# The last pooling products at set places, the first projection groups in pairs, and LayerNorm's TensorE steps 12 to 24 products sooner

## The chip, the cores and the metric

The kernel runs on one core of one Trainium2 chip. The metric is the device time of one launch in microseconds (us), taken as the median of three runs: 1085.06 us before the change, from 1084.37 to 1085.12.

## What is computed

One layer of a decoder trunk, in float32, on 288 tokens: 256 of a prompt and 8 x 4 sampled ones. Cut to what matters:

```python
h = rmsnorm(x, norm1_g)                                   # 2048 channels
proj = h @ w_in + b_in
a, gate, z = proj[:, :1024], proj[:, 1024:2048], proj[:, 2048:]
u = a * sigmoid(gate)                                     # after the history of 30 tokens
c = silu(layernorm(depthwise_conv31(u), ln_g, ln_b))
d = mean of z over windows of 2, 4, 8, 16 tokens (one a group of 256 channels) - z
p = (d of each group @ pool_w of the group) * pool_scale
x = x + concat(c, p) @ w_out                              # 2048 x 2048
x = x + relu(rmsnorm(x, norm2_g) @ w_ff1) ** 2 @ w_ff2    # 2048 x 8192 x 2048
y = rmsnorm(x, norm_f)
```

## The kernel before

Channels lie on the 128 partitions, tokens in the free dimension. Each float32 operand of a large product is split into a high part (`whi`, `hh`) that TensorE's float32r keeps, and the rest (`wlo`, `hl`); of the four partial products three are taken. So every product here is one matmul of 128 x 128 weights with 128 x 288 moving values, and all that matters below is called a *product* in that sense.

A group of products is one call of `gemm(banks, rhs)`. Weights come in blocks of 512 KB: SP's queue loads a block (`load`), ScalarE casts the high part (L274), VectorE or GpSimd subtracts for the low part (L279, L282). `ready` holds the weight groups that are already asked for; `gemm` takes the first one and, when it has recorded its products, asks for one more. The stages stand in `SEQUENCE`: c0 to c7 are the eight convolution groups (96 products each, `a` and `gate` of 128 channels), p3 to p0 the projections of the pooling groups, P3 to P0 the 12 products of each pooling group with its own weights (`pool_products`, tile `pp`). The names of the tail are these:

- *g0 to g7*, the first half of `w_out`: eight groups of 48 products each, moving operand `mixp` (tiles `dx`, what `pool_products` wrote), two accumulating banks a group from the pool `acc`, which has room for two groups. VectorE adds the banks to `xT` (L587).
- *h0 to h7*, the second half of `w_out`: eight groups of 48, moving operand `mixc` (tiles `mx`), added at L609.
- *ff1, ff2*: 64 groups of 96 products, 6,144 in all.

LayerNorm needs TensorE three times, and the three places are inside g5 to g7 by `BETWEEN`: `ln_mean` (tile `pmean`, two matmuls in full float32, which take two passes each), `ln_sums` (three thin matmuls into `pt`, L246, then root and reciprocal on ScalarE and VectorE, L249 to L256), and `ln_rows` (three matmuls that spread the result, `pt<-ident,st`). Then VectorE multiplies (`n`, L592), ScalarE does SiLU (L595) and the cast (`mx`, L597), VectorE the low part (L598).

The order of TensorE's instructions comes from two things. While the list `chain` is not empty, `mm` ties every matmul behind the last, so that it stands where the program's text has it. When it is empty, a list scheduler places each instruction by its own estimate. Before the change the chain is given up at P1 (`chain.clear()` at L541), so P1, P0, g0, g1, h0 and h1 lie where the scheduler put them.

A moving operand's high and low parts lie in one tile of four rows of 288 values (L122, `rows`): high parts in rows 1 and 2, low parts in rows 0 and 3. The six products of a pair of channel blocks on one bank read the rows 1, 2, 1, 2, 0, 3: even and odd rows alternate, when nothing comes in between. The string `TURN` is an order for the first 48 products of a group, in which the parity of the row is 1,1,0,1,0,0 four times, then 0,1 six times, then 1,1,0,0 three times; `classes=TURN` reorders the head of a group to it (L332). Before the change it stands in the first stages, at c5, in g2, h2 and in the second group of ff1.

Of the kernel before, what the change touches and what calls it, by code (L numbers as in the profile page):

```python
# [86 lines left out]
def trunk_kernel(ctx: ExitStack, tc: tile.TileContext, io):  # L87
# [46 lines left out]
    def f32(t):  # L134
        return t.bitcast(F32)
# [71 lines left out]
    def load_table(func, src):  # L207

        return nc.scalar.activation(few[: src.shape[0], :], src, func)
# [97 lines left out]
            chain[0] = last.ins  # L307
        return last

    def gemm(banks, rhs, m_outer=False, between={}, classes="", by_part=False):  # L310


        n = len(rhs)
        gets = ready.pop(0)
        todo, begins = [], {}
        if by_part:
            for k in range(0, n, 2):
                sets = [range(len(banks))] if k else [range(2), range(2, len(banks))]
                for last, ms_ in enumerate(sets, 1 - len(sets)):
                    for part, (w, x) in enumerate(((0, 0), (1, 0), (0, 1))):  # L320
                        if last == 0:
                            begins[len(todo)] = (k, None, k + 1)[part]
                        todo += [(k + (1 - d if x else d), m, w, x) for m in ms_ for d in range(2)]
        else:
            pairs = [(k, m) for k in range(0, n, 2) for m in range(len(banks))]
            if m_outer:
                pairs.sort(key=lambda km: km[1])
            for k, m in pairs:
                if m == 0:
                    begins[len(todo)] = k  # L330
                todo += [(k + d, m, w, x) for d, w, x in ((0, 0, 0), (1, 0, 0), (0, 1, 0), (1, 1, 0), (1, 0, 1), (0, 0, 1))]
        head = todo[: len(classes)]  # L332
        for j, c in enumerate(classes):
            todo[j] = next(p for p in head if (p[0] + p[3]) % 2 == int(c))
            head.remove(todo[j])
        ends = {m: [f(j for j, p in enumerate(todo) if p[1] == m) for f in (min, max)] for m in range(len(banks))}
        ahead = None
        for j, (k, m, w, x) in enumerate(todo):
            if begins.get(j) in between:
                ahead = between[begins[j]]()  # L340
            with tc.issue_after(ahead.ins) if ahead is not None and not chain else nullcontext():
                last = mm(banks[m][:, :T], gets[k // 8](k % 8, m)[w], rhs[k][x], start=j == ends[m][0], stop=j == ends[m][1])
        ready.extend(itertools.islice(weights, 1))
        return last.ins
# [4 lines left out]
    def each(bk):  # L349
        return [bk[:, m, :] for m in range(2)]  # L350
# [83 lines left out]
    def conv_products(i, **kw):  # L434
        history(i)
        banks = each(bank2())
        gemm(banks, hx, **kw)
        return banks

    def conv_pair(i, banks):  # L440
        up = u_all[:, i, 0:UO]
        us = samples(u_all[:, i, UO:UL], US)
        ta, gate = [b[:, :T] for b in banks]
        for b in (gate, ta):
            nc.vector.tensor_tensor(b, b, rb, op=ALU.mult)
        tg = tmpp.tile([P, 2, T], F32, name=nm("tg"), tag="ag", bufs=2)[:, 0, :]
        nc.scalar.activation(tg, gate, AF.Sigmoid, bias=v("b_in", 8 + i))
        for out, a, b in ((up[:, CH:UO], ta[:, :SEQ], tg[:, :SEQ]), (us[:, :, CH:US], samples(ta[:, SEQ:T], NS), samples(tg[:, SEQ:T], NS))):
            nc.vector.scalar_tensor_tensor(out=out, in0=a, scalar=v("b_in", i), in1=b, op0=ALU.add, op1=ALU.mult)
        if i % 2 == 0:  # L450
            cs.append(actp.tile([P, 2, T], F32, name=nm("c"), tag="c", bufs=4))
        c = cs[i // 2][:, i % 2, :]
        with later():
            if i % 2 == 0:
                pcs.append(cvp.tile([P, 2, SEQ], F32, name=nm("pc"), tag="cv"))
            pc = pcs[i // 2][:, i % 2, :]
            cwv = vec[:, CWO + i * CW : CWO + (i + 1) * CW]
            nc.scalar.activation(pc, up[:, 0:SEQ], AF.Identity, bias=v("conv_b", i), scale=cwv[:, 0:1])  # L458
            for w in range(1, CW):
                dst = pc if w < CW - 1 else c[:, 0:SEQ]  # L460
                nc.vector.scalar_tensor_tensor(out=dst, in0=up[:, w : w + SEQ], scalar=cwv[:, w : w + 1], in1=pc, op0=ALU.mult, op1=ALU.add)  # L461
            prd = prdp.tile([P, NB, NS, CW + 1], F32, name=nm("prd"), tag="prd")
            nc.scalar.activation(prd[:, :, :, CW], ones[:, 0 : NB * NS].rearrange("p (b t) -> p b t", t=NS), AF.Identity, bias=v("conv_b", i), scale=0.0)
            nc.gpsimd.tensor_tensor(prd[:, :, :, 0:CW], windows(us, CW), cwv[:, None, None, :].to_broadcast([P, NB, NS, CW]), op=ALU.mult)
            cso = c[:, SEQ:T]
            nc.vector.tensor_reduce(samples(cso, NS), prd, axis=AX.X, op=ALU.add)
            if i % 2 and 1 < i < N8 - 1:
                for m in range(2):
                    nc.gpsimd.tensor_tensor(sum_c[:, m, :], (cs[0] if i == 3 else sum_c)[:, m, :], cs[i // 2][:, m, :], op=ALU.add)
            if i == N8 - 2:  # L470
                for part in (sum_c[:, 1, :], c):
                    nc.gpsimd.tensor_tensor(sum_c[:, 0, :], sum_c[:, 0, :], part, op=ALU.add)
# [35 lines left out]
    def pool_products(g):  # L508

        bk = ms("pp")  # L510
        gemm(each(bk), halves(dd[g]))
        for m, (mh, ml) in enumerate(halves(dd[g])):
            i = 2 * g + m
            nc.scalar.activation(mh, bk[:, m, :T], AF.Copy, scale=v("pool_scale", i))
            nc.vector.scalar_tensor_tensor(out=ml, in0=bk[:, m, :T], scalar=v("pool_scale", i), in1=f32(mh), op0=ALU.mult, op1=ALU.subtract)
            mixp[i] = (mh, ml)
# [19 lines left out]
    conv_pair(0, pair0)  # L536
    conv_pair(1, pair1)
    conv_pair(2, third)
    for kind, i in SEQUENCE[3:]:
        if (kind, i) == ("P", 1):  # L540
            chain.clear()  # L541
        if kind == "c":
            conv_pair(i, conv_products(i, classes=TURN if i == 5 else ""))
        elif kind == "p":
            pool_group(i)
        else:
            pool_products(i)
    load_table(AF.Sqrt, f32(mixp[1][0])[:, 0:1])
    with later(2 * LATER):
        nc.sync.dma_start(io["u_out"], u_all[:, :, UO - CH : UL])  # L550
# [25 lines left out]
        norm["rows"], last = spread(norm["sums"])  # L576
        return last

    BETWEEN = {5: {4: ln_mean}, 6: {6: ln_sums}, 7: {2: ln_rows}}
    behind = nullcontext()  # L580
    for g in range(8):
        bk = bank2()
        with behind:
            last = gemm(each(bk), [mixp[k] for k in korder], between=BETWEEN.get(g, {}), classes=TURN if g == 2 else "")
        behind = tc.issue_after(last) if g > 3 else nullcontext()
        x2 = xT[:, 2 * g : 2 * g + 2, :]
        nc.vector.tensor_tensor(x2, x2, bk[:, :, :T], op=ALU.add)  # L587
# [13 lines left out]

    x1 = []
    ss2 = row("ss2")
    last = None
    for g in range(8):
        bk = bank2()
        last = gemm(each(bk), mixc, classes=TURN if g == 2 else "")
        x2 = xT[:, 2 * g : 2 * g + 2, :]
        nc.vector.tensor_tensor(x2, x2, bk[:, :, :T], op=ALU.add)  # L609
        if g < 4:  # L610
            a2 = halves(act2("ax", tag="p", bufs=4))
        elif g < 6:
            if g == 4:
                ax45 = zp.tile([P, N8 * ZL], F32R, name="ax45", tag="z")
                ax45 = ax45[:, 32 : 32 + 8 * T].rearrange("p (g r t) -> p g r t", g=2, r=4)
            a2 = halves(rows(ax45[:, g - 4]))
        else:
            a2 = []
            for m in range(2):
                t2 = actp.tile([P, 2, T], F32R, name=nm("ax"), tag="c", bufs=4)  # L620
                a2.append((t2[:, 1 - m, :], t2[:, m, :]))
        for m, (ah, al) in enumerate(a2):
            k = 2 * g + m
            xk = xT[:, k, :]
            nc.scalar.activation(ah, xk, AF.Copy, scale=v("norm2_g", k))
            nc.vector.scalar_tensor_tensor(out=al, in0=xk, scalar=v("norm2_g", k), in1=f32(ah), op0=ALU.mult, op1=ALU.subtract)
            x1.append((ah, al))
            if k == 0:
                nc.scalar.activation(ss2, xk, AF.Square)
            else:  # L630
                q2 = tmp("q")
                nc.scalar.activation(q2, xk, AF.Square)
                nc.gpsimd.tensor_tensor(ss2, ss2, q2, op=ALU.add)
# [150 lines left out]
```

## Time and profile before

| | |
|---|---|
| median of 3 runs | 1085.06 us (1084.37, 1085.06, 1085.12) |
| span of the profiled execution, first to last instruction | 1082.8 us |
| TensorE busy | 1071.5 us, 8198 matmul records |
| VectorE, ScalarE, GpSimd busy | 635.4, 479.0, 173.6 us |
| granted TensorE clock, mean | 0.997 |
| P1 to the end of h2, the part that the change touches | 159.8 to 239.1 us of the span |

No time of its own is given for the profiled execution beside its span; the three runs lie 1.6 to 2.3 us above it. TensorE counts as busy for nearly the whole span whatever it does, because the records of matmuls overlap (about 0.29 us each, one begun every 0.13 us). So its busy share says little here, and what is to be read is the time from one product's start to the next.

### The profile page before, as it was taken

Reading aid. Unit: us, or ns where it says so; the run is one execution under the profiler, and the core shown is the slowest. Engines: PE = TensorE matmul, PEld = TensorE weight load, DVE = VectorE, ACT = ScalarE, POOL = GpSimd, SP = SyncE. Lnnn points to the kernel's source line nnn. Section 1 sums busy time; section 2 is a strip of 40 time slices with the busy share of each in tenths; the row PEclk is TensorE's granted clock in tenths of the full one; section 3 lists DMA queues with packets and bytes.
Section 4 is the critical chain, followed back from the end, with each engine's and each line's share of the span. In section 5 each row is a group of like instructions: output and inputs, shape, how many; then the busy total and the mean of one; then the engine's idle time right before and its main releaser. Section 6 shows DMA issues by size and latency. Waiting matters only on the chain.

```text
span 1082.8 us, 19572 instructions
## 1 busy us (share of the span) xinstructions
PE 1071.5 (99%) x8198; PEld 1069.9 (99%) x8198; DVE 635.4 (59%) x818; ACT 479.0 (44%) x585; POOL 173.6 (16%) x180
## 2 busy tenths in 40 slices
PE   9999999999999999999999999999999999999996
PEld 9999999999999999999999999999999999999996
DVE  8899999678655544445544444545544445554553
ACT  8654445475544433334443333444433334444441
POOL 0878979512000000000000000000000000000001
PEclk9999999999999999999999999999999999999998
DMA  9896468545555555555555555555555555555522
GB/s 325 281 273 185 137 196 239 176 152 177 173 164 170 172 166 169 174 164 169 171 168 168 175 165 169 174 167 167 174 165 168 174 169 165 173 166 168 173 78 88
DMA packets 58296, 190.71 MB, mean 176 GB/s; under 512 B 6240, under 2 KB 11232, under 8 KB 58208
## 3 DMA queue, kind: packets, MB, share of 16 engines
q1 hardware_dynamic: 56336, 184.35, 53.9%
q0 software_dynamic: 1008, 3.67, 1.9%
q8 instruction: 64, 1.05, 0.4%
q10 hardware_dynamic: 864, 1.44, 0.4%
q14 instruction: 24, 0.20, 0.1%
HBM read 185.16 MB, written 4.28 MB: 175 GB/s over the span
## 4 chain that ended last, share of the span: by engine, by line
PE 77%; issue 20%; ACT 1%; DVE 0%; DMA 0%; POOL 0%; POOLq 0%
PE ac L305 77%; PE pp L305 1%; DMA wr<-in_w 0%; ACT whi L274 0%; POOL xT L720 0%; ACT n L595 0%; DVE wlo L279 0%; PE pt L305 0%; PE pmean L305 0%; POOLq L770 0%; DVE xT L695 0%; DVE n L592 0%; ACT whi L364 0%; ACT mx L597 0%; DVE hx L367 0%
## 5 line engine op out<-in xcount | busy, mean ns | idle before, releaser
L274 ACT CAST whi<-wr 128x1024 fp32r<-128x1024 f32 (+1 forms) x332 | 348.0, 1049 | 551.4 <-PE ac L305 533.5
L279 DVE TENSOR_TENSOR wlo<-wr,whi 128x1024 fp32r<-128x1024 f32 x288 | 353.1, 1226 | 348.5 <-ACT whi L274 348.5
L305 PE MATMUL ac<-ax,whi 128*128 128x288 f32 x2048 | 351.0, 292 | 0.0
L305 PE MATMUL ac<-fx,whi 128*128 128x288 f32 x2048 | 350.2, 292 | 0.0
L305 PEld LDWEIGHTS ac<-ax,whi 128*128 128x128 f32 x2048 | 296.0, 187 | 0.0
L305 PEld LDWEIGHTS ac<-fx,whi 128*128 128x128 f32 x2048 | 295.6, 187 | 0.0
L305 PE MATMUL ac<-ax,wlo 128*128 128x288 f32 x1024 | 217.4, 292 | 0.0
L305 PE MATMUL ac<-fx,wlo 128*128 128x288 f32 x1024 | 216.4, 292 | 0.0
L305 PEld LDWEIGHTS ac<-ax,wlo 128*128 128x128 f32 x1024 | 162.6, 187 | 0.0
L305 PEld LDWEIGHTS ac<-fx,wlo 128*128 128x128 f32 x1024 | 162.3, 187 | 0.0
L305 PE MATMUL ac<-hx,whi 128*128 128x288 f32 x768 | 131.8, 295 | 1.2 <-DVE hx L367 1.2
L720 POOL TENSOR_TENSOR xT<-xT,rf 128x288 f32<-128x288 f32 x4 | 3.1, 795 | 800.1 <-ACT rf L724 800.1
L305 PEld LDWEIGHTS ac<-hx,whi 128*128 128x128 f32 x768 | 112.1, 190 | 1.4 <-ACT hx L369 1.4
L282 POOL TENSOR_TENSOR wlo<-wr,whi 128x512 fp32r<-128x512 f32 x74 | 100.3, 1410 | 35.3 <-ACT whi L274 34.3
L461 DVE SCALAR_TENSOR_TENSOR pc<-u_all,vec,pc 128x256 f32<-128x256 f32 x232 | 99.5, 483 | 1.9 <-ACT pc L458 0.7
L305 PE MATMUL ac<-hx,wlo 128*128 128x288 f32 x384 | 80.1, 294 | 0.0
L305 PEld LDWEIGHTS ac<-hx,wlo 128*128 128x128 f32 x384 | 61.1, 190 | 0.0
L305 PE MATMUL ac<-dx,whi 128*128 128x288 f32 x256 | 46.0, 296 | 0.0
L305 PE MATMUL ac<-mx,whi 128*128 128x288 f32 x256 | 45.1, 294 | 0.1
L664 DVE SCALAR_TENSOR_TENSOR t<-ac,r 128x576 f32<-128x576 f32 x32 | 24.2, 758 | 25.1 <-PE ac L305 25.1
L305 PEld LDWEIGHTS ac<-dx,whi 128*128 128x128 f32 x256 | 38.0, 188 | 0.2
L305 PEld LDWEIGHTS ac<-mx,whi 128*128 128x128 f32 x256 | 37.5, 188 | 0.6 <-ACT mx L597 0.4
(133 smaller groups left out, 533.6 us busy)
## 6 DMA issues: line engine op xcount, KB each, us to landing
wr<-in_w SPq DMA_DIRECT2D x335, 512.0 KB, 3.8
wlo<-in_w POOLq DMA_DIRECT2D x7, 512.0 KB, 7.7
xT<-in_xT SPq DMA_DIRECT2D x8, 288.0 KB, 7.3
wr<-in_w SPq DMA_DIRECT2D x5, 256.0 KB, 3.6
out_u_out<-u_all SPq DMA_DIRECT2D x1, 1208.0 KB, 9.3
u_all<-in_hist_c SPq DMA_DIRECT2D x8, 136.0 KB, 6.2
out_z_out<-z_all SPq DMA_DIRECT2D x1, 668.0 KB, 9.9
z_all<-in_hist_p SPq DMA_DIRECT2D x4, 152.0 KB, 7.5
```

What stands on the lines that cost most here:

```text
L274: nc.scalar.copy(hi, raw)
L279: nc.vector.tensor_tensor(lo, raw, f32(hi), op=ALU.subtract)
L282: nc.gpsimd.tensor_tensor(lo[:, j : j + 2, :], raw[:, j : j + 2, :], f32(hi[:, j : j + 2, :]), op=ALU.subtract)
L305: last = nc.tensor.matmul(*args, **kw)
L461: nc.vector.scalar_tensor_tensor(out=dst, in0=up[:, w : w + SEQ], scalar=cwv[:, w : w + 1], in1=pc, op0=ALU.mult, op1=ALU.add)
L664: nc.vector.scalar_tensor_tensor(out=t, in0=bk[:, :, :T], scalar=0.0, in1=both(rows2[0]), op0=ALU.max, op1=ALU.mult)
L720: eng.tensor_tensor(xk, xk, r[:, None, :].to_broadcast([P, n, T]), op=ALU.mult)
```

## The change

1. `pool_products(1)` (P1) is put between the products of c7, ahead of channel block 12, by `between`; the weights of c7 are taken from `ready` by the new function `ahead`.
2. g0 and g1 become one call of `gemm` with four banks. Its order is: blocks 0, 2 and 4 of g0 (36 products), P0, blocks 0, 2, 4 of g1, then block 6 of both. Behind P0 the 48 products follow `TURN`. The chain is given up after this call instead of at P1, and `TURN` leaves g2.
3. `ln_mean` moves from block 4 to block 0 of g5 (24 products), `ln_sums` from block 6 to 4 of g6 (12), `ln_rows` from block 2 to 0 of g7 (12). g5 and g7 get `TURN` behind these steps.
4. h0 and h1 become one call with four banks, tied behind g7 by the chain; h2 keeps its `TURN`.

```diff
-        gets = ready.pop(0)
+        gets = gets or ready.pop(0)
...
-            pairs = [(k, m) for k in range(0, n, 2) for m in range(len(banks))]
+            pairs = pairs or [(k, m) for k in range(0, n, 2) for m in range(len(banks))]
...
-                if m == 0:
-                    begins[len(todo)] = k
+                begins[len(todo)] = (k, m) if m else k
...
-            todo[j] = next(p for p in head if (p[0] + p[3]) % 2 == int(c))
+            todo[j] = next(p for p in head if c == "." or (p[0] + p[3]) % 2 == int(c))
...
-    for kind, i in SEQUENCE[3:]:
+    def ahead(n):
+
+        while len(ready) < n + 1:
+            ready.extend(itertools.islice(weights, 1))
+        return ready.pop(n)
+
+    for kind, i in SEQUENCE[3:-1]:
         if (kind, i) == ("P", 1):
-            chain.clear()
+            continue
         if kind == "c":
-            conv_pair(i, conv_products(i, classes=TURN if i == 5 else ""))
+            conv_pair(i, conv_products(i, classes=TURN if i == 5 else "", **(dict(gets=ahead(1), between={12: lambda: pool_products(1)}) if i == 7 else {})))
...
+    proj = [halves(dd[k // 2])[k % 2] for k in korder]
+    bks = [bank2() for _ in range(2)]
+    both_gets = [ahead(1) for _ in range(2)]
+    early = [(k, m) for k in (0, 2, 4) for m in range(4)]
+    early.sort(key=lambda km: km[1] // 2)
+    gemm(each(bks[0]) + each(bks[1]), proj, gets=[lambda k, m: both_gets[m // 2][0](k, m % 2)], between={(0, 2): lambda: pool_products(0)}, classes="." * 36 + TURN, pairs=early + [(6, m) for m in range(4)])
+    chain.clear()
...
-    BETWEEN = {5: {4: ln_mean}, 6: {6: ln_sums}, 7: {2: ln_rows}}
+    BETWEEN = {5: {0: ln_mean}, 6: {4: ln_sums}, 7: {0: ln_rows}}
...
-        bk = bank2()
-        with behind:
-            last = gemm(each(bk), [mixp[k] for k in korder], between=BETWEEN.get(g, {}), classes=TURN if g == 2 else "")
+        bk = bks[g] if g < 2 else bank2()
+        if g > 1:
+            with behind:
+                last = gemm(each(bk), proj, between=BETWEEN.get(g, {}), classes=TURN if g in (5, 7) else "")
...
-    last = None
+    chain.append(last)
+    bks = [bank2() for _ in range(2)]
+    two_gets = [ahead(0) for _ in range(2)]
+    gemm(each(bks[0]) + each(bks[1]), mixc, gets=[lambda k, m: two_gets[m // 2][0](k, m % 2)])
+    chain.clear()
     for g in range(8):
-        bk = bank2()
-        last = gemm(each(bk), mixc, classes=TURN if g == 2 else "")
+        bk = bks[g] if g < 2 else bank2()
+        if g > 1:
+            last = gemm(each(bk), mixc, classes=TURN if g == 2 else "")
```

From the end of h2 on, and before c7, the order of instructions is the same on every engine; SP's and GpSimd's queues keep their order throughout, so no transfer changes its place among the others. Three places show what moves.

TensorE, P1 in c7 (tile `ac` is c7's bank, `hx` the normalized input, `pp` and `dx_1877` belong to P1). Before:

```order
L305 MATMUL ac_2089<-hx_215,whi_2075 128x288
L305 MATMUL pp_2044<-dx_1877,whi_2023 128x288 x2
L305 MATMUL pp_2044<-dx_1877,wlo_2024 128x288 x2
L305 MATMUL ac_2089<-hx_215,whi_2075 128x288
L305 MATMUL ac_2089<-hx_227,whi_2080 128x288 x2
L305 MATMUL ac_2089<-hx_227,wlo_2081 128x288 x2
L305 MATMUL ac_2089<-hx_227,whi_2080 128x288
L305 MATMUL pp_2044<-dx_1877,whi_2023 128x288 x4
```

And in the changed kernel:

```order
L305 MATMUL ac_2072<-hx_215,whi_2062 128x288 x2
L305 MATMUL pp_2145<-dx_1877,whi_2023 128x288 x2
L305 MATMUL pp_2145<-dx_1877,wlo_2024 128x288 x2
L305 MATMUL pp_2145<-dx_1877,whi_2023 128x288 x4
L305 MATMUL pp_2145<-dx_1877,wlo_2024 128x288 x2
L305 MATMUL pp_2145<-dx_1877,whi_2023 128x288 x2
L305 MATMUL ac_2072<-hx_227,whi_2067 128x288 x2
```

P1 no longer splits a pair of blocks in the middle; rows 1, 2, 1, 2, 0, 3 stay whole, and even and odd alternate through it.

TensorE, the start of g1 (before: bank `ac_2265` is g0's, `ac_2329` is g1's, `pp_2233` is P0's). Before:

```order
L305 MATMUL pp_2233<-dx_2041,whi_2188 128x288 x2
L305 MATMUL ac_2265<-dx_1877,whi_2250 128x288 x4
L305 MATMUL ac_2265<-dx_1877,wlo_2251 128x288 x2
L305 MATMUL ac_2265<-dx_1877,whi_2250 128x288 x2
L305 MATMUL ac_2265<-dx_2041,whi_2250 128x288
L305 MATMUL ac_2329<-dx_1246,whi_2323 128x288 x2
L305 MATMUL ac_2329<-dx_1246,wlo_2324 128x288 x2
```

In the changed kernel (`ac_2245` is g0's bank, `ac_2246` g1's, `pp_2297` P0's):

```order
L305 MATMUL ac_2245<-dx_1877,whi_2196 128x288 x2
L305 MATMUL pp_2297<-dx_2041,whi_2160 128x288 x2
L305 MATMUL pp_2297<-dx_2041,wlo_2161 128x288 x2
L305 MATMUL pp_2297<-dx_2041,whi_2160 128x288 x4
L305 MATMUL pp_2297<-dx_2041,wlo_2161 128x288 x2
L305 MATMUL pp_2297<-dx_2041,whi_2160 128x288 x2
L305 MATMUL ac_2246<-dx_1246,whi_2256 128x288
L305 MATMUL ac_2246<-dx_1246,wlo_2257 128x288
L305 MATMUL ac_2246<-dx_1246,whi_2256 128x288 x2
```

P0 now stands right ahead of g1, and g1 begins in the order of `TURN`.

VectorE, from the thin sums to the first `mx` (`st` are the small root tiles, `wlo` low parts of weights). Before:

```order
L249 TENSOR_SCALAR st_2709<-pt_2705 96x3
L253 RECIPROCAL st_2709<-st_2709 96x3
L254 TENSOR_TENSOR st_2709<-st_2709 96x3
L255 SCALAR_TENSOR_TENSOR st_2709<-st_2709 96x3
L256 SCALAR_TENSOR_TENSOR st_2709<-st_2709 96x3
L587 TENSOR_TENSOR xT<-xT,ac_2652 128x576
L279 TENSOR_TENSOR wlo_2892<-wr_2887,whi_2891 128x1024
L592 TENSOR_TENSOR n_2809<-c_638,pt_2705 128x576
```

In the changed kernel, whose lines from about L330 on have other numbers:

```order
L249 TENSOR_SCALAR st_2711<-pt_2707 96x3
L279 TENSOR_TENSOR wlo_2752<-wr_2745,whi_2751 128x1024
L253 RECIPROCAL st_2711<-st_2711 96x3
L254 TENSOR_TENSOR st_2711<-st_2711 96x3
L255 SCALAR_TENSOR_TENSOR st_2711<-st_2711 96x3
L256 SCALAR_TENSOR_TENSOR st_2711<-st_2711 96x3
L600 TENSOR_TENSOR xT<-xT,ac_2666 128x576
L605 TENSOR_TENSOR n_2821<-c_638,pt_2707 128x576
```

A weight's low part now stands inside the root chain, and the one that stood ahead of the first `n` is behind it.

More of the change, by code (lines that the diff above doesn't have):

```diff
@@ L308, in mm, with gemm @@
         return last
-    def gemm(banks, rhs, m_outer=False, between={}, classes="", by_part=False):
+    def gemm(banks, rhs, m_outer=False, between={}, classes="", by_part=False, gets=None, pairs=None):
         n = len(rhs)
-        gets = ready.pop(0)
+        gets = gets or ready.pop(0)
         todo, begins = [], {}
```

## The prediction

> **What bounds the kernel.** I read the page first: the busy shares and the chain of work that ended last.
>
> ```profile
> span 1082.8 us, 19572 instructions
> PE 1071.5 (99%) x8198; PEld 1069.9 (99%) x8198; DVE 635.4 (59%) x818; ACT 479.0 (44%) x585; POOL 173.6 (16%) x180
> PEclk9999999999999999999999999999999999999998
> PE 77%; issue 20%; ACT 1%; DVE 0%; DMA 0%; POOL 0%; POOLq 0%
> ```
>
> TensorE has work throughout, at full clock, and the chain rests on it. So two things only can change the time: how far apart products start, and the few waits of TensorE. The table of stretches gives the first (length, busy time, matmuls that touch the stretch, clock, DMA share, GB/s):
>
> ```profile
> 186.05:198.53 12.48, 12.48 (x98) 1.00 0.54 178
> 203.45:210.11 6.66, 6.66 (x53) 1.00 0.55 170
> 300.00:1060.00 760.00, 760.00 (x5848) 1.00 0.53 165
> ```
>
> Matmuls that only overlap an edge are counted too, so I take the number of products from the order: 96 in the first stretch (130.0 ns each), 50 in the second (133.2 ns), 5,846 in the third (130.0 ns). Same tile, clock and DMA, but two spacings. The timeline of TensorE shows where they lie (start, duration of the row's products together, count at the end):
>
> ```profile
> 159.81 0.43 PE L305 MATMUL pp<-dx,whi 128*128 128x288 f32 x2
> 165.24 0.70 PE L305 MATMUL ac<-dx,whi 128*128 128x288 f32 x4
> 167.64 0.70 PE L305 MATMUL ac<-dx,whi 128*128 128x288 f32 x4
> 170.84 0.97 PE L305 MATMUL ac<-dx,whi 128*128 128x288 f32 x5
> 178.94 0.56 PE L305 MATMUL ac<-dx,whi 128*128 128x288 f32 x3
> 179.34 0.29 PE L305 MATMUL ac<-dx,wlo 128*128 128x288 f32 x1
> 185.41 0.56 PE L305 MATMUL ac<-dx,whi 128*128 128x288 f32 x3
> 201.15 0.65 PE L305 MATMUL pmean<-sum_c,ones 128*128 128x288 f32 x2
> 201.63 0.65 PE L305 MATMUL pmean<-c,ones 128*128 128x288 f32 x2
> 201.90 0.65 PE L305 MATMUL ac<-dx,whi 128*128 128x288 f32 x2
> 210.11 0.59 PE L305 MATMUL pt<-ones,q 128*96 128x1 f32 x6
> 210.56 0.51 PE L305 MATMUL ac<-dx,whi 128*128 128x288 f32 x2
> 213.82 0.80 PE L305 MATMUL pt<-ident,st 96*128 96x96 f32 x6
> 214.41 0.51 PE L305 MATMUL ac<-dx,whi 128*128 128x288 f32 x2
> 219.00 0.43 PE L305 MATMUL ac<-dx,whi 128*128 128x288 f32 x2
> 219.55 0.54 PE L305 MATMUL ac<-mx,whi 128*128 128x288 f32 x2
> 232.47 0.61 PE L305 MATMUL ac<-mx,whi 128*128 128x288 f32 x3
> 239.63 0.68 PE L305 MATMUL ac<-mx,whi 128*128 128x288 f32 x4
> ```
>
> From 165.24 to 167.64 lie 18 products in 2.40 us, 133.3 ns. The slow spacing begins where P1 splits a pair of blocks in the middle and so breaks the alternation of even and odd rows; it ends in g2, whose head has `TURN` (from 179.34 to 185.41 46 products take 6.07 us, 0.09 more than 46 x 0.13), and from 186.05 on the spacing is 130.0. It begins again behind `pmean` and ends in h2, which has `TURN` as well. I read it so: an order with alternating rows keeps the short spacing, a break loses it, 48 products of `TURN` restore it for about 0.10 us. Ahead of 219.55 TensorE stood 0.28 us (the two products begun at 219.00 would have been followed at 219.27). The waits for `mx` and `xT` between 156 and 246 us (us in total, times, longest):
>
> ```profile
> PEld ac L305 <- ACT mx L597: 0.4, 1, 0.4
> PEld ac L305 <- DVE xT L587: 0.2, 1, 0.2
> ```
>
> **The floor.** From the product behind P1's start (159.81 + 0.13 = 159.94) to the end of h2's `TURN` (four products ahead of 239.63: 239.11) are 576 products, 74.88 us at 0.13, and LayerNorm's three steps: 0.75 (201.15 to 201.90), 0.45 (210.11 to 210.56), 0.59 (213.82 to 214.41), together 76.67. Before it took 79.17. So no more than 2.5 us can be won at all.
>
> **The parts.** *P1 whole, up to g1.* At 130.0 ns the 84 products from P1 to g1 (P1 12, c7 24, g0 36, P0 12) take 10.92 us, so that g1 could begin at 170.86 instead of 171.27 (in the row at 170.84 the fourth of five starts there; it is 0.97 long where four otherwise take 0.70 and one more adds 0.13: it waited some 0.13). But g1's bank is one of c7's, and is free when VectorE has written `u_all` (second row below):
>
> ```profile
> 164.91 1.47 DVE L503 TENSOR_TENSOR dx<-d,dx 128x576 fp32r<-128x576 f32 x1
> 170.58 0.64 DVE L449 SCALAR_TENSOR_TENSOR u_all<-ac,vec,tg 128x256 f32<-128x256 f32 x2
> ```
>
> It ends at 171.22. VectorE has no gap from P1's start to there (length, VectorE's busy time, its operations, clock, DMA share, GB/s):
>
> ```profile
> 159.81:171.22 11.41, 11.41 (x24) 1.00 0.76 232
> ```
>
> Its queue is filled with the depthwise convolution and sets that moment, whether c7's products end 0.1 us sooner or not. So the 0.41 us become a wait at g1, and what is late next is VectorE. Behind it come 60 products to g2 at 0.13 (7.80), `TURN` (0.10) and a restart of 0.10 like the one seen: 171.27 + 8.00 = 179.27; before g2 began at 179.20 (third product of the row at 178.94). +0.07. P0 ends 0.8 us later than before, and block 6 of g0, 36 products behind g1's start, needs its low part: a wait of 0 to 0.4; I take 0, since by its old place behind P0 it comes with little to spare.
>
> *g2 to g4.* Before 179.20 to g5's start, 201.15 - 24 x 0.13 = 198.03: 18.83. Without `TURN` in g2 144 x 0.13 = 18.72. -0.11, if the short spacing has come back in g0 and g1.
>
> *LayerNorm's steps sooner.* Their own cost stays. What feeds them, and what hangs on them:
>
> ```profile
> 195.80 0.48 DVE L461 SCALAR_TENSOR_TENSOR c<-u_all,vec,pc 128x256 f32<-128x256 f32 x1
> 208.94 0.46 DVE L571 TENSOR_TENSOR q<-q 128x288 f32<-128x288 f32 x1
> 209.84 1.23 DVE L279 TENSOR_TENSOR wlo<-wr,whi 128x1024 fp32r<-128x1024 f32 x1 [0.44 <-ACT whi L274]
> 210.99 0.15 DVE L249 TENSOR_SCALAR st<-pt 96x3 f32<-96x3 f32 x1
> 211.41 0.17 DVE L253 RECIPROCAL st<-st 96x3 f32<-96x3 f32 x1 [0.27 <-ACT st L250]
> 212.00 0.16 DVE L256 SCALAR_TENSOR_TENSOR st<-st 96x3 f32<-96x3 f32 x1
> 219.47 0.76 DVE L587 TENSOR_TENSOR xT<-xT,ac 128x576 f32<-128x576 f32 x1 [0.33 <-PE ac L305]
> 220.14 1.42 DVE L598 TENSOR_TENSOR mx<-n,mx 128x576 fp32r<-128x576 f32 x2
> 218.84 1.23 ACT L597 CAST mx<-n 128x576 fp32r<-128x576 f32 x2
> ```
>
> `pmean` now stands at 198.0; the last `c` ends at 196.28, 1.7 us ahead of it. From `pmean` to `ln_sums` VectorE needs 201.90 to 209.40, 7.50 us; now 72 products lie between, 9.36 us and more, so 1.9 us remain. From `ln_sums` to `ln_rows` 24 products remain, 3.2 us and the step's 0.45. The root chain ran from 210.11 to 212.16, 2.05, of which VectorE stood 0.27 for ScalarE's root; a `wlo` of 1.23 now stands in that gap: 3.0 against 3.65. That holds by 0.6. This is the tightest place, since the `wlo` waits in its turn for ScalarE's `whi` (0.44 in its row), and the root operations are queued behind it; if that waits 0.44 and the `wlo` is slowed as well, up to 0.4 comes to stand on TensorE. I take 0, since 0.44 alone fits. From `ln_rows` to the first product on `mx` 48 products lie now, at least 6.24 us behind the step's end. The high part came 5.05 behind it (half of the cast's row, 219.46, less 214.41), the low part 6.49 (220.90), needed 0.5 later, with a `wlo` and the `xT` ahead of it that no longer wait there. So the 0.28 us that TensorE stood before 219.55 goes. From g5's start to the first `mx` product: 144 x 0.13 = 18.72, the steps 1.79, `TURN` twice 0.20, 24 products between `ln_sums` and `ln_rows` at the slow spacing 0.08, and what is lost in the first products behind each step, 0.22 + 0.09 + 0.09: 21.2 together. Before 198.03 to 219.55 = 21.52. -0.34.
>
> *h0 and h1 as a pair.* Before 219.55 to 232.74 (third product of the row at 232.47): 13.19, which is 96 x 0.1333 and 0.39 of waits for `mx` and `xT`. Now 96 x 0.13 = 12.48 and, for the last `xT` of g7 in VectorE's queue, 0 to 0.1: 12.53. -0.66. h2 with its `TURN`: 6.34 against 6.37, -0.03.
>
> *Weights.* `ahead` asks for the same blocks in the same row on SP and GpSimd, so no transfer is moved past another. ScalarE's and VectorE's work on them is the same in number; its only new place with a follower is the `wlo` above. I price this at nothing; if blocks came late at the pairs, where four banks draw on two groups at once, the cost would be up to a low part and the cast ahead of it, put as long: twice 1.23, about 2.5 us, once.
>
> Sum: 0.07 - 0.11 - 0.34 - 0.66 - 0.03 = -1.07; with a small wait in one of the three bounded places (0.4, 0.4, 0.1), -1.0. Against the span 1082.8 that is 1081.8. The median 1085.06 lies 2.26 above that span, which I leave as it is: **1084.1 us**. Of its own this case has 1083.6 to 1085.2 (1084.0 with no wait to 1084.8 with all of them, and half of the runs' spread of 0.75 on either side).
>
> **Rivals.** (a) *VectorE does not hold g1.* The `dx` operation took 1.47 us beside GpSimd's work; an operation of its size took 0.76 (`xT`).
>
> ```profile
> 164.47 8.09 POOL L282 TENSOR_TENSOR wlo<-wr,whi 128x512 fp32r<-128x512 f32 x6 [1.77 <-ACT whi L274]
> ```
>
> If it falls ahead of that stretch, `u_all` comes 0.7 sooner, g1 begins at 170.86, g2 at 178.76, and the sum is -1.6: 1083.5. The Trainium skill, "SBUF — State Buffer", section "Who interferes with whom", says that a VectorE operation with two inputs in SBUF contends with a GpSimd operation that reads SBUF; the 1.47 against 0.76 agrees. Against (a): it needs ScalarE's part sooner too, and that hangs on the same queue. Chance 0.13.
>
> (b) *The short spacing does not come back in the pair or behind the steps.* `TURN` starts behind a wait of 0.4 us in g1, and the wait for P0's low part would fall inside it; before, `TURN` met no wait in g2 and h2. If all stays at 133.3 until h2, g2 begins 0.17 later, g2 to g4 take 0.37 more, LayerNorm gains 0.14 and the h pair 0.39: 0.0, so 1085.1. Chance 0.22.
>
> (c) *The slower side: the short spacing is lost beyond h2.* The order from there on is the old one, but should `TURN` in h2 not catch what the new h pair leaves, and the one in ff1 neither, every product in the long stretch costs 3.3 ns more: 5,846 x 3.3 ns = 19 us, about 1103. It cancels the gain from 300 products on, and makes 0.2% from some 960. For it speaks that nothing else changes so much with so little; against it, that both heads restored it before. Chance 0.05.
>
> (d) *Order has no price,* and 130 or 133 belongs to the place. Then 130 does not come at P1, g1's wait stays 0.13, and what goes are waits: 0.28 before `mx` and 0.39 in h0 and h1: -0.67, so 1084.4. Against it: both spacings stand in the same g groups, with the change just at the steps. Chance 0.03. The Trainium skill, "TensorE: Matmul & The Clock Gate", section "Back-to-back issue gap", gives one gap for a width, N/2.4 + 2.5 ns when warm for a single matmul (an estimate of 122.5 ns at 288), and names no order of rows; the trace has 130.0 and 133.3 at that width, so that the rule doesn't settle it.
>
> **The numbers.** Forecast 0.57, (a) 0.13, (b) 0.22, (c) 0.05, (d) 0.03. A measurement of this kernel can tell about 0.2%, 2.17 us, from no change: faster would mean below 1082.9, which only nearly the whole floor gives: 0.05, from the tail of (a). Slower is (c) and a late block: 0.06. Same: 0.89. The range 1083.0 to 1085.8 holds (a) to (b) with half a microsecond on either side for the runs' spread.
>
> **What will show it.** Right: 130.0 ns from P1 on, a stop of 0.3 to 0.5 us at g1's first product with `u_all` as its releaser, g2's start near 179.3, no wait at the first `mx`, h2's start about 1.0 sooner. Wrong: 133 ns in g2 to g4 (b), g1 at 170.9 (a), a stop ahead of `pt<-ident` (the `wlo` in the root chain), or 133 ns behind 240 us (c).

## The result, and the profile after

The changed kernel takes 1083.53 us, the median of 21 runs (1082.39 to 1085.16); the kernel before, in 21 runs beside it, 1085.02 (1083.77 to 1086.06). The ratio is 0.9987, 95% interval 0.9982 to 0.9993: 1.4 us less, between 0.8 and 2.0. That was forecast as a gain of 1.0 us, to 1084.1, in a range of 1083.0 to 1085.8. The gain is clear of zero, but under the 0.2% (2.17 us) that the forecast took for the least that counts as a change.

The page and the table of stretches, of the kernel after:

```profile
span 1081.2 us, 19573 instructions
PE 1069.8 (99%) x8198; PEld 1068.7 (99%) x8198; DVE 636.8 (59%) x818; ACT 477.6 (44%) x585; POOL 174.6 (16%) x180
178.86:197.58 18.72, 18.72 (x147) 1.00 0.65 208
218.69:231.24 12.55, 12.55 (x99) 1.00 0.53 165
300.00:1060.00 760.00, 760.00 (x5848) 1.00 0.53 165
```

The span is 1.6 us shorter. g2 to g4 (first of the three stretches: 144 products) and h0 with h1 (second: 96 products) now run at 130.0 ns but for 0.07 us in the second; the long stretch is what it was. The starts of the parts, TensorE's timeline:

```profile
160.04 0.42 PE L305 MATMUL pp<-dx,whi 128*128 128x288 f32 x2
170.96 0.29 PE L305 MATMUL ac<-dx,whi 128*128 128x288 f32 x1
178.60 0.68 PE L305 MATMUL ac<-dx,whi 128*128 128x288 f32 x4
197.58 0.65 PE L305 MATMUL pmean<-sum_c,ones 128*128 128x288 f32 x2
208.44 0.51 PE L305 MATMUL ac<-dx,whi 128*128 128x288 f32 x2
211.70 0.81 PE L305 MATMUL pt<-ident,st 96*128 96x96 f32 x6
218.69 0.42 PE L305 MATMUL ac<-mx,whi 128*128 128x288 f32 x2
220.00 0.74 PE L305 MATMUL ac<-mx,whi 128*128 128x288 f32 x4
230.98 0.56 PE L305 MATMUL ac<-mx,whi 128*128 128x288 f32 x3
237.43 0.56 PE L305 MATMUL ac<-mx,whi 128*128 128x288 f32 x3
```

P1 begins at 160.04, g1 at 170.96, g2 at 178.86 (third product of the row at 178.60), g5's step at 197.58, the first product on `mx` at 218.69, h2 at 231.24, and h2's `TURN` ends at 237.57. Against the starts of before:

| from, to | before | after | difference | forecast |
|---|---|---|---|---|
| P1, g1 | 11.33 | 10.92 | -0.41 | 0 |
| g1, g2 | 7.93 | 7.90 | -0.03 | +0.07 |
| g2, `ln_mean` (g5) | 18.83 | 18.72 | -0.11 | -0.11 |
| g5, first product on `mx` | 21.52 | 21.11 | -0.41 | -0.34 |
| h0 and h1 | 13.19 | 12.55 | -0.64 | -0.66 |
| h2 with `TURN` | 6.37 | 6.33 | -0.04 | -0.03 |
| sum | 79.17 | 77.53 | -1.64 | -1.07 |

The sum of the right places is the whole difference of the spans; ahead of P1 (0.10 us more) and behind h2 (0.06 less) nothing of size changed. The term that was forecast wrongly is the first, and with it 0.10 of the second, the restart that was to follow a wait at g1.

### The profile page after: what moved, and what is told of

The parts are those of the page before. It is cut to its first block, busy times and chain, and to the rows that moved or that the text cites. A ratio compares the mean times of both kernels' runs of the same rounds, so it can differ in the third digit from the quotient of the medians.

```text
span 1081.2 us, 19573 instructions
## 1 busy us (share of the span) xinstructions
PE 1069.8 (99%) x8198; PEld 1068.7 (99%) x8198; DVE 636.8 (59%) x818; ACT 477.6 (44%) x585; POOL 174.6 (16%) x180
## 4 chain that ended last, share of the span: by engine, by line
PE 76%; issue 20%; DMA 2%; DVE 1%; ACT 0%; POOL 0%; SPq 0%; POOLq 0%; DVEq 0%
PE ac L305 75%; DMA wr<-in_w 1%; PE pp L305 1%; DMA u_all<-in_hist_c 0%; DVE wlo L279 0%; POOL xT L738 0%; PE pt L305 0%; ACT whi L363 0%; DVE hx L375 0%; DVE st L255 0%; DVE wlo L372 0%; PE pmean L305 0%; ACT hx L368 0%; SPq L191 0%; POOLq L788 0%
```

## Experiments

Below, "the stretch" is the time from P1's first product to the end of h2's 48 products: 79.17 us before (counted there from the product at 159.94, so that both hold 576 products), 77.53 after. A profile shows it to some hundredths; a single time scatters by about 1 us, so times are used only where several us are at stake or there are eleven runs.

**Two casts exchanged on ScalarE.** In the kernel after, ScalarE casts a weight block (`whi`, then GpSimd's `wlo`) ahead of P0's `dx`; before it was the other way round. The two rows before, then the two after:

```profile
162.78 0.67 ACT L502 CAST dx<-d 128x576 fp32r<-128x576 f32 x1
163.34 1.05 ACT L274 CAST whi<-wr 128x1024 fp32r<-128x1024 f32 x1
162.20 1.05 ACT L274 CAST whi<-wr 128x1024 fp32r<-128x1024 f32 x1
163.14 0.68 ACT L501 CAST dx<-d 128x576 fp32r<-128x576 f32 x1
```

In this run only that is put back (`late` is the `dx` cast for the first block of w1, and empty otherwise):

```diff
-        nc.scalar.copy(dh, d)
+        dx_cast[g] = nc.scalar.copy(dh, d).ins
...
-        nc.scalar.copy(hi, raw)
+        with tc.issue_after(late) if late is not None else nullcontext(): nc.scalar.copy(hi, raw)
```

> The changed kernel with one thing exchanged on ScalarE: the cast of P0's dx ahead of a weight cast, as in the kernel before. Theory (which of the two casts comes first decides whether VectorE's dx operation runs beside GpSimd's subtraction): GpSimd's subtraction begins near 164.4 instead of 163.3, the dx operation takes about 1.47 us instead of 0.75, u_all is written near 171.3 instead of 170.6, and g1's first product waits 0.3 us; from P1's first product to the end of h2's TURN 77.85 instead of 77.53. Rival 1 (the 1.47 us had another cause, or chance): 0.75 us again, no wait, 77.5. Rival 2 (TURN does not work behind a wait): 133.3 ns from g1 to g5, 0.3 + 0.8 more, 78.6.

First the kernel after (VectorE twice, GpSimd twice), then this run:

```profile
165.03 0.75 DVE L502 TENSOR_TENSOR dx<-d,dx 128x576 fp32r<-128x576 f32 x1
169.99 0.63 DVE L448 SCALAR_TENSOR_TENSOR u_all<-ac,vec,tg 128x256 f32<-128x256 f32 x2
163.32 1.72 POOL L282 TENSOR_TENSOR wlo<-wr,whi 128x512 fp32r<-128x512 f32 x1 [0.51 <-ACT whi L274]
165.01 1.92 POOL L282 TENSOR_TENSOR wlo<-wr,whi 128x512 fp32r<-128x512 f32 x1
```

```profile
164.39 1.43 DVE L502 TENSOR_TENSOR dx<-d,dx 128x576 fp32r<-128x576 f32 x1
163.92 1.29 POOL L282 TENSOR_TENSOR wlo<-wr,whi 128x512 fp32r<-128x512 f32 x1 [1.74 <-ACT whi L274]
165.17 1.81 POOL L282 TENSOR_TENSOR wlo<-wr,whi 128x512 fp32r<-128x512 f32 x1
170.81 0.37 PE L305 MATMUL ac<-dx,whi 128*128 128x288 f32 x1 [0.34 <-DVE u_all L448]
```

In this run VectorE's `dx` begins 0.47 us into a GpSimd subtraction, which keeps its 1.29, and takes 1.43; the next subtraction takes 1.81. In the kernel after it begins at the border of two subtractions (165.03 and 165.01) and takes 0.75, and the GpSimd operation 1.92 in its place. So one runs at a time, and the order on ScalarE decides which of them pays. It is no accident of one execution: `dx` took 0.74 to 0.85 in all twelve profiles with the new order on ScalarE. The difference of 0.7 us reaches TensorE: `u_all` ends 0.3 us before g1 would begin at 170.96 (169.99 + 0.63 = 170.62), here 0.35 behind the due 170.31 (P1 at 159.39, 84 products); g1 begins 0.50 late and its second product another 0.07. The stretch takes 78.41 us, 0.88 more: 0.57 of that is this wait (forecast 0.3); most of the rest is the long spacing in h0 and h1, of which below. `TURN`, behind the wait, worked: 130.0 ns from 177.25 on. Rivals 1 and 2 fall.

**One swap, and one full-float32 step, in the feed-forward.** No `TURN` stands behind either. `swap` is set for the first group of ff2's first quarter:

```diff
+        if swap:
+            todo[4], todo[5] = todo[5], todo[4]
```

> The changed kernel with two neighbouring products exchanged once, in the first pair of blocks of ff2's first group (the rows then go odd, even, odd, even, even, odd, odd, even: two repeats). No TURN comes behind it. 56 groups of 96 products follow. Theory A (any repeat of a row's parity loses the short spacing for good): 5,370 x 3.3 ns = 17.7 us more, about 1101. Theory B (only a gap in the stream loses it: a wait, a full-float32 step, a thin product): within 0.1 us of the changed kernel, 1083.5. Rival C (the spacing mends itself): 133 ns for some groups, then 130 again, in between.

```diff
-        mm(mean, means, hi, start=True, stop=False)
-        last = mm(mean, means, lo, start=False, stop=True)
+        last = mm(mean, f32(means), ss2, start=True, stop=True)
...
-            gemm(..., classes="01" * 6 + TURN if ch == 0 and g == 1 else "")
+            gemm(...)
```

> The changed kernel with the mean of squares ahead of the feed-forward taken by one full-float32 matmul (two passes) instead of two products, like LayerNorm's mean, and without the TURN behind it. Theory: the long spacing from there to the end, some 6,000 products x 3.3 ns = 20 us more, about 1103.5. Rival (a loss is local and mends itself within a few groups): under 1 us, 1083 to 1084.5.

They took 1101.96 and 1102.96 us. Stretches ahead of the swap (the first row) and behind it (the second), and behind the full-float32 step (the third):

```profile
300.00:369.00 69.00, 69.00 (x533) 1.00 0.53 169
400.00:1060.00 660.00, 660.00 (x4952) 1.00 0.51 164
300.00:1060.00 760.00, 760.00 (x5702) 1.00 0.52 165
```

4,950 products in 660.00 us are 133.3 ns; the long spacing begins at the swap, near 370 us. Two neighbours exchanged once cost 17.9 us (from h2's end to the last instruction 861.5 us, in the kernel after 843.6; forecast 17.7), since nothing brings the short spacing back. Behind the full-float32 step it holds from 284 us to the end. This is the strongest test of the reading on which the prediction rests: it is a state, the order of rows sets it, and it doesn't mend of itself (theory B and rival C fall, and with them case (d), that order has no price). By the Trainium skill, "TensorE: Matmul & The Clock Gate", section "Back-to-back issue gap", the gap of a single matmul follows from its width (N/2.4 + 2.5 ns when warm). Here 288 columns have 130.0 or 133.3 at the same clock of 1.00 for 660 us and more on end, so the width alone does not set it. The row order told ahead, 1, 2, 1, 2, 0, 3, is the one that the swap makes; the code has 1, 2, 1, 2, 3, 0, and that alternates. A digit 1 of `TURN` stands for an even row, 0 for an odd one. `TURN` repeats parities itself, so "a repeat loses the short spacing" is no full rule: shown is that this swap loses it and that `TURN` brings it back.

**Without `TURN`.** First at four places where the spacing just ahead of it was 130.0:

```diff
-            conv_pair(i, conv_products(i, classes=TURN if i == 5 else "", **(...)))
+            conv_pair(i, conv_products(i, **(...)))
...
-    gemm(..., between={(0, 2): lambda: pool_products(0)}, classes="." * 36 + TURN, pairs=...)
+    gemm(..., between={(0, 2): lambda: pool_products(0)}, pairs=...)
...
-            last = gemm(each(bk), mixc, classes=TURN if g == 2 else "")
+            last = gemm(each(bk), mixc)
...
-            gemm(..., classes="01" * 6 + TURN if ch == 0 and g == 1 else "")
+            gemm(...)
```

> The changed kernel without TURN at the four places where its trace shows products 130.0 ns apart just ahead of the order: c5, the pair g0 and g1, h2, and the second group of ff1. Theory (the spacing is a state that only a break in the row order or a full-float32 step loses, and that stays of itself): 130.0 ns through all four places, and the time that each TURN took above 48 x 0.13 us goes, 4 x 0.10 = 0.4 us; span 1080.8, median near 1083.1. Rival 1 (the set order itself keeps the spacing, and without it it decays): 133.3 ns from c5 on or from one of the places on; between the pair and g5 that is 240 x 3.3 ns = 0.8 us, behind ff1 some 5,850 x 3.3 ns = 19 us. Rival 2 (order has no price): no change of the time, within 0.1 us of the span of the changed kernel, 1081.2.

Of 13 executions five took 1082.7 to 1086.0 and eight 1105.2 to 1108.0 us, all at a granted clock of 0.996 to 0.998. The profile is of one of the eight; its waits, TensorE and VectorE at h1, and two stretches:

```profile
PEld ac L305 <- DVE dx L514: 0.2, 1, 0.2
220.29 0.75 PE L305 MATMUL ac<-mx,whi 128*128 128x288 f32 x4
219.70 0.75 DVE L600 TENSOR_TENSOR xT<-xT,ac 128x576 f32<-128x576 f32 x1
177.07:196.27 19.20, 19.20 (x147) 1.00 0.67 215
300.00:1060.00 760.00, 760.00 (x5702) 1.00 0.52 165
```

Neither the theory nor the rivals had it right. The spacing is 130.0 ns until a product waits: 0.2 us in the pair for P0's low part, and from there 133.3 up to g5's `TURN`; then some 0.06 us in the row at 220.29 (four products 0.75 long instead of 0.68), and from there 133.3 to the end. That last wait is in the kernel after too (the row at 220.00), is ahead of h1's first product (the third of the row, at 220.55 here), and follows VectorE's `xT` of g7, whose bank h1 takes: it ends at 220.45. There the short spacing outlived it; in the runs of the two casts, the swap and the full-float32 step it did not, and h2's `TURN` brought it back. So a wait of 0.06 us loses it at times, and `TURN` is a guard behind places that may wait. The last two of these ran on the same chip as the two runs that follow, so a difference of chips does not explain what comes.

If so, the eight executions must go once that wait goes, guards or not. h1 begins 12 products later:

```diff
-    gemm(each(bks[0]) + each(bks[1]), mixc, gets=[...])
+    gemm(each(bks[0]) + each(bks[1]), mixc, gets=[...], pairs=[(k, m) for h in (0, 2) for k in (0, 2) for m in (h, h + 1)] + [(k, m) for k in (4, 6) for m in range(4)])
```

> The changed kernel without TURN in c5, h2 and ff1 (the pair keeps its own), and with h1's first product 12 products later: blocks 0 and 2 of h0, then blocks 0 and 2 of h1, the rest as it was. In the run without four TURNs the long spacing began at the product that waited some 0.06 us for h1's bank (VectorE's xT of g7) and never ended. Theory (a wait, however short, may lose the short spacing, and nothing else did here): no wait at h1, 130.0 ns from there to the end without any guard, no execution above 1086, span 1080.8, median near 1083.1. Rival 1 (TURN is needed at times whatever waits, the spacing decays): again many executions near 1105 to 1108. Rival 2 (the second mx tile, now needed 1.56 us sooner, is late): a wait of up to 0.5 us ahead of block 2, and the long spacing behind it, 20 us in most executions.

> The same order of h0 and h1, with TURN kept in the pair, in g5, g7, h2 and ff1, and left out in c5 alone. Theory: 0.06 us (the wait for h1's bank) and 0.10 (TURN in c5) less than the changed kernel: span 1081.0, median 1083.4, no execution above 1085.5. Rival (the second mx tile is late): up to 0.5 us more, but caught by TURN in h2: 1083.9 to 1084.2.

No execution above 1086.3 in the first, none above 1086.8 in the second: the 20 us are gone with the wait. But in both, seven of eleven took 1085.1 or more, and four 1082.0 to 1083.8, so that the medians, 1085.28 and 1085.63, missed the forecast 1083.1 and 1083.4. Stretches and a row of TensorE of the unguarded run, and a weight load of the guarded one:

```profile
83.25:160.00 76.75, 76.75 (x578) 1.00 0.56 168
220.85:239.57 18.72, 18.72 (x147) 1.00 0.47 155
300.00:1060.00 760.00, 760.00 (x5848) 1.00 0.51 165
50.15 0.48 PE L305 MATMUL ac<-hx,wlo 128*128 128x288 f32 x2
76.44 0.30 PEld L305 LDWEIGHTS ac<-hx,wlo 128*128 128x128 f32 x2 [0.29 <-DMA wlo<-in_w]
```

From h0 on all is 130.0. The long spacing lies in the convolution groups (576 products in 76.75 us): it begins at a short wait (in the unguarded run some 0.06 us in the row at 50.15, two products 0.48 long instead of 0.42; in the guarded run 0.3 us for a DMA that fetches a low part) and lasts to the pair, 915 products and 3.0 us from 51 to 173 us in the unguarded profile. c5's `TURN`, left out in both, is the guard there: in the kernel after, a wait of 0.1 us near 79 us begins the long spacing as well, and from the end of that `TURN`, near 92 us, it is 130.0 again. Last, with it kept:

> The order in which h1 begins 12 products later, TURN kept in c5, the pair, g5 and g7, and left out in h2 and the second group of ff1. In the two runs without TURN in c5 a wait of 0.05 to 0.5 us somewhere between 48 and 82 us began the long spacing, which then lasted to the pair, up to 3 us; so c5's TURN stays. Theory: no wait and no break lies between g7's TURN and the end of the feed-forward, so nothing has to be restored there; against the changed kernel two TURNs (0.20 us), the wait at h1 (0.06) and, where that wait began the long spacing, 0.25 us up to h2 go: span 1080.7 to 1081.0, median 1083.2, no execution above 1085.5. Rival (some execution loses the short spacing behind h2 without a wait that the profile shows): single executions between 1086 and 1104.

> The changed kernel with all its TURNs and h1 12 products later. Theory: the wait at h1's first product (0.06 us) goes, and with it the 0.25 us of long spacing up to h2 that three of five profiles showed behind it; end of h2's TURN 77.47 us behind P1's first product, median 1083.4. Rival (the second mx tile, needed sooner, waits in some executions): 77.5 to 78.0.

The first (no guard in h2 and ff1) took 1083.15 us, 1082.65 to 1083.96 in 11 runs, ratio to before 0.9987 (0.9978 to 0.9996). The second (all guards, only h1 later) took 1082.93, 1082.17 to 1084.42, ratio 0.9984 (0.9975 to 0.9992); its stretch is 77.46 us, forecast 77.47. Neither can be told from the changed kernel, whose ratio is 0.9987 too: their medians are lower than its 1083.53, but so is that of the kernel before beside them, 1084.65 against 1085.02. What is shown is that without a wait at h1 no guard is needed behind it: 22 unguarded executions with h1 later had no loss behind it, 13 with h1 at once had eight.

**LayerNorm's places and its `TURN`s, each alone.** The first run has only the first of these edits, the second both:

```diff
-                last = gemm(..., classes=TURN if g in (5, 7) else "")
+                last = gemm(...)
...
-    BETWEEN = {5: {0: ln_mean}, 6: {4: ln_sums}, 7: {0: ln_rows}}
+    BETWEEN = {5: {4: ln_mean}, 6: {6: ln_sums}, 7: {2: ln_rows}}
```

> The changed kernel without TURN in g5 and g7, all steps at their new places. Theory: 133.3 ns from behind the mean to h2; against the changed kernel 72 and 144 products at 3.3 ns more, less two TURNs: 0.24 + 0.48 - 0.20 = 0.5 us more at the end of h2's TURN (237.57 - 160.04 = 77.53 us from P1's first product becomes 78.05). The first product on mx 21.2 us behind the mean instead of 21.11. Rival (the short spacing comes back of itself or belongs to the place): 0.2 us less, 77.33.

> The changed kernel with LayerNorm's three steps at their old places (24, 36 and 12 products into g5, g6 and g7) and without TURN in g5 and g7: against the run without these two TURNs it tells what the places alone are worth. Theory: a wait of about 0.28 us ahead of the first product on mx and 0.3 to 0.4 us behind it, so some 0.6 us more than that run, less 24 products in the slow spacing (0.08): 78.5 us from P1's first product to the end of h2's TURN. Rival (the steps' work was hidden, only the spacing counted): the same as that run, 78.0.

The stretch is 77.98 us without the two `TURN`s (forecast 78.05), and 79.16 with the old places as well (forecast 78.5). The waits of the second:

```profile
PEld ac L305 <- DVE mx L611: 0.8, 1, 0.8
PEld ac L305 <- ACT mx L610: 0.3, 1, 0.3
```

So the places are worth 1.2 us here, not 0.6: the paired h0 and h1 wait 0.8 us for the first low part of `mx`, which stands behind other work in VectorE's queue.

**Half of the change, and the pairing of h0 and h1 alone.** In both runs h0 and h1 are left to the scheduler, as before the change; the first also has the old `BETWEEN` and no `TURN` in g5 and g7:

```diff
-    chain.append(last)
-    bks = [bank2() for _ in range(2)]
-    two_gets = [ahead(0) for _ in range(2)]
-    gemm(each(bks[0]) + each(bks[1]), mixc, gets=[...])
-    chain.clear()
+    last = None
...
-        bk = bks[g] if g < 2 else bank2()
-        if g > 1:
-            last = gemm(each(bk), mixc, classes=TURN if g == 2 else "")
+        bk = bank2()
+        last = gemm(each(bk), mixc, classes=TURN if g == 2 else "")
```

> The first two parts of the change alone: P1 and P0 at set places, g0 and g1 paired, TURN in the pair; LayerNorm's steps, h0 and h1 as before. Theory: the terms of this stretch in the two profiles, -0.41 (P1 to g1), -0.03 (g1 to g2), -0.11 (g2 to g5), and then the old 21.5, 13.2 and 6.4: 79.17 - 0.55 = 78.6 us from P1's first product to the end of h2's TURN. Rival (LayerNorm's steps, now sooner, wait for c or for VectorE and give it back): 79.0 to 79.2.

> The changed kernel with h0 and h1 left to the scheduler, as before the change (the rest unchanged): what the pairing alone is worth. The scheduler begins h1 behind two blocks of h0 but splits a pair of blocks twice. Theory: no wait at h1; the long spacing from the first split on, some 66 products up to h2, 0.2 us more: 77.7 us from P1's first product to the end of h2's TURN. Rival (the pairing took away the waits for mx and xT): 0.4 us more, 77.9 to 78.0.

The first two parts alone give 78.63 us (forecast 78.6), 0.54 of the 1.64. With the steps sooner but h0 and h1 unpaired it is 77.60 (forecast 77.7): 1.03 less than with the first two parts, and 0.07 more than in the changed kernel. With the old places the pairing even costs 0.5 us (79.16 against 78.63). What was booked as the pairing's gain is for the most part the steps' gain: the pairing adds next to nothing of its own.

## Why the prediction came out as it did

The mechanism was right and is now shown by experiment: the time is the spacing of products, and row order holds or loses the short one. The terms for g2 to g4, h2 and the h pair came within 0.02 us. For the h pair that is luck in part: its 0.66 was booked for pairing h0 and h1, and the pairing alone is worth 0.07; the rest comes with the steps. LayerNorm's term was 0.07 too small, with no stop ahead of `ln_rows`, the place called tightest: its step begins 3.26 us behind the products of `ln_sums`, as before.

The step that failed is "So the 0.41 us become a wait at g1, and what is late next is VectorE". It is a mis-sized term: the wait at g1 measured 0, not 0.41, and the restart of 0.10 behind it fell away too. VectorE does set that moment, as the run with the casts exchanged shows; but its length was carried over from before with the 1.47 us of the `dx` row in it. The numbers are those of case (a), given a chance of 0.13 (g1 10.92 us behind P1, as forecast there; 1083.5), but the road is another. Case (a) had `dx` come sooner, ahead of GpSimd's subtractions, and against it stood that it "needs ScalarE's part sooner too". In fact `dx` came no sooner: it begins 4.99 us behind P1's start (165.03 against 160.04), before 4.97. GpSimd came sooner, at 163.32 instead of 164.47, because ScalarE cast the weight first, and so `dx` met the border of two subtractions. The prediction took ScalarE's and GpSimd's rows from before and did not ask in which order they would come now.

The other cases: (b) `TURN` was feared not to work behind a wait; it did, behind 0.5 us. What the case did hold is a loss inside h0 and h1: they take 12.81 us instead of 12.55 in the runs of the two casts, the swap and the full-float32 step. (c) had the mechanism and the price right (18 to 21 us in the three profiles that lost it, forecast 19), and the changed kernel is kept from it by the guards in h2 and ff1. (d) is refuted by the swap. P0's low part caused no wait at g0's last block: `TURN` puts that product later; without `TURN` it waited 0.2 us. The measured 1083.53 lies just under the forecast's own range, 1083.6 to 1085.2, and inside the whole one; that it lies so near is luck too, for a term of 0.51 us was missed, and single executions scatter by more than that.

What stays open: by what the state is held, and why one and the same wait of 0.06 us loses it in one execution and not in another. The first distance behind that wait already differs: 126 ns in the kernel after, 133 in the run without the four `TURN`s.

## What to carry to other kernels

Where one engine bounds the kernel without a gap, list the starts of its instructions: a second spacing that begins at one instruction and then stays is a state, and what is to be sought is the instruction at which it begins. A short wait there may cost some 350 times its own length (0.06 us led to 21), so it is worth more to keep products off banks and tiles that come free at the last moment than to shorten the order that mends the loss. And when an instruction order moves, read it on the helper engines too: here two casts on ScalarE decided 0.6 us on TensorE.

## What was not expected of the hardware

- A wait of 0.06 us, once, led to 133.3 ns instead of 130.0 for the next 6,500 products or so: 21 us.
- Two neighbouring products exchanged, once, cost 17.9 us of 1083.5.
- At the short spacing single starts lie 128 to 132 ns apart, in turn. At the long one three distances of about 131 ns are followed by one of about 140: in the swap's profile, from 400 to 1060 us, 1,237 of 4,949 distances are above 138 ns, each four products behind the last. So one product in four pays 9 ns, not each of them 3.3.
- VectorE's two-operand subtraction and GpSimd's run one after the other: 0.75 or 1.43 us for the one, 1.29 or 1.92 for the other, by which of them is running when the other comes. The Trainium skill, "SBUF — State Buffer", section "Who interferes with whom", says that a VectorE instruction with two inputs in SBUF contends with a GpSimd instruction that reads SBUF. The traces agree: 1.43 us for one begun 0.47 us into a GpSimd subtraction, 0.75 for one begun at the border of two.
